# A diffusion layer on one core: third feature block's weight sums written two token steps later, second spilled chunk read back into a weight buffer

## The chip, the cores and the metric

The kernel runs on one core of one Trainium2 chip. The metric is the time of one execution on the device in microseconds (us), as the median of several runs; lower is better.

## The reference, cut to what matters

The reference is one layer of a diffusion backbone in float32: 512 latent tokens and 256 context tokens of width 1024. Each passes a gated feed-forward block, then attention and a short convolution, then a second feed-forward block. The change lies in the first feed-forward block (FFN 1, 2816 hidden features = 22 blocks of 128):

```python
def swiglu(x, w_gate, w_up, w_down):
    return (jax.nn.silu(x @ w_gate) * (x @ w_up)) @ w_down

def ffn_sublayer(h, mods, pre_g, post_g, w_gate, w_up, w_down):
    shift, scale, gate = mods
    y = swiglu(modulate(rms_norm(h, pre_g), shift, scale), w_gate, w_up, w_down)
    return h + 0.5 * gate * rms_norm(y, post_g)
```

`shift`, `scale` and `gate` come from a matrix product of the conditioning vector with `w_mod`, so the tokens can only be modulated when that product is there.

## The kernel before, in words

**Number format.** Each float32 operand of a matmul is split in two: a rounded part (`hi`, a cast on ACT, line 64) and the rest (`lo`, a subtraction, on DVE unless said otherwise, line 69). A product is then three matmuls: hi·hi, hi·lo, lo·hi.

**Start.** The 768 tokens lie transposed, as eight blocks of 128 features (k = 0 to 7). The modulation is made in four pieces of two k-blocks each: `mod_mm(i)` multiplies on PE, `mod_col(i)` turns the row into columns (eight small matmuls `pd<-pick,row` at line 351, then DVE additions into `mst` at line 356 and `s1` at line 360). `mod_x(d)` then scales block d: DVE multiplies the latent tokens (line 370), ACT adds the shift (372), POOL multiplies the context tokens (374), ACT finishes those (375), then hi and lo. `mod_t(p)` forms sums and differences of two token blocks, four products (lines 399 to 402), on POOL for p below 3, on DVE for p = 3; `mod_tp(p)` splits them into hi and lo.

The 22 hidden blocks are called f = 0 to 21. For f = 0 and 1, `open_steps` runs plain products: one `next(first)` is all matmuls (36) of one k-block. From f = 2 on, a product with seven instead of eight sub-products per 2x2 block is used. It needs sums of the weights as well: `w_load(f)` issues the two raw loads (512 KB each), `w_pool(f)` makes two sums on POOL (lines 464, 465), `w_dve(f)` two on DVE (lines 470, 471; the first needs line 464's result, and both read the raw gate weights), `w_hi(f, i)` and `w_lo(f, i)` split operand i (0 and 1 raw, 2 and 3 sums). The sum buffers `s12` and `s4` exist once each. `begin(f)` opens a block on PE, `product` is a sub-product (line 668), `plain_tail` applies Silu (line 650, with a load of ACT's table before the first) and product for f = 0 and 1 and spills the chunk.

**Order.** PE, DVE, ACT and POOL keep the order of the program text inside `with self.in_order()`. DMAs are all issued from SP; the order there is set by the framework's scheduler, as buffers come free. Inside the loop over i = 0 to 3 (lines 525 to 544), an iteration writes: k-block 2i; then for i below 3 `mod_col(i + 1)`, `mod_x` of two blocks, `mod_tp(i)`, `mod_t(i + 1)`; then k-block 2i + 1; for i below 2 `mod_mm(i + 2)`; and in i = 1 everything of f = 2's weight work that doesn't need more buffers.

**Spill and down.** Every finished hidden block f, 128 x 768 tokens as hi and lo, is written to HBM: the latent part to `hl_dram[f]` (512 KB), the context part to `hc_dram[f]`. Down (`down`, lines 764 to 789) then reads them back block by block (`fetch`, two ahead) together with a weight block `f1d[f]`, and adds into eight banks: 24 matmuls per chunk f (line 787). The chunks' read buffers are two "h" in the pool `hp`, which lives on from gate/up, and two "h2" in `fp`, which takes the memory that the gate/up pools leave at `sa.close()`. Chunk 0 is read before that (lines 740, 741) into "h", chunk 1 by `fetch(1)` into "h2". Weight blocks come through four raw buffers "wraw" of 128 x 1024, the same size as a chunk, and are split into four hi/lo pairs. Beside down's latent half DVE accumulates further modulation rows (`mod_acc`, lines 564 to 582, four steps per chunk from chunk 1 on; loads `mraw`). After it comes the context half over `hc_dram`, with the normalisation of the latent rows beside it (`sandwich`, lines 1286 to 1330).

Of the kernel before, what the change touches and what calls it, by code (L numbers as in the profile page):

```python
# [9 lines left out]
F32R = mybir.dt.float32r  # L10
# [6 lines left out]
P = 128  # L17
DM = 1024
ND = 8
NT = 512  # L20
# [19 lines left out]
class Builder:  # L40
# [153 lines left out]
    def build(self):  # L194
# [56 lines left out]
        hl_dram = self.t(dp, [NF, P, 2, NT], "hl_dram", F32R)  # L251
# [47 lines left out]
        def load_gu(f):  # L299
            out = []  # L300
            for i in range(2):
                raw = self.t(self.wp, [P, DM], "wraw", bufs=self.n_raw)
                nc.sync.dma_start(out=raw, in_=io["f1gu"][f, i])
                out.append(raw)
            return out
# [3 lines left out]
        def ring():  # L309

            i = nring[0] % 6
            nring[0] += 1
            if i < 4:
                return [self.t(self.wp, [P, DM], tag, F32R, bufs=self.n_hl) for tag in ("whi", "wlo")]
            return [self.t(fa, [P, DM], tag, F32R, bufs=2) for tag in ("whx", "wlx")]
# [89 lines left out]
        def mod_tp(p):  # L405
            u, v = tsum.pop(p)
            t12[p] = [slot(2 * p + hl, [P, 2, HK], F32R) for hl in range(2)]
            t34[p] = [self.t(fa, [P, 2, HK], "wm", F32R, bufs=8) for hl in range(2)]
            for (h, l), w in ((t12[p], u), (t34[p], v)):
                self.hi(h, w)  # L410
                self.lo(l, w, h)
# [42 lines left out]
        def w_load(f):  # L454
            rg, ru = load_gu(f)
            s12 = self.t(fa, [P, 2, 512], "s12")
            s4 = self.t(fa, [P, 512], "s4")
            wop[f] = [rg, ru, s12, s4]
            wsrc[f] = rg, ru, s12, s4

        def w_pool(f):
            rg, ru, s12, s4 = wsrc[f]
            tt = nc.gpsimd.tensor_tensor
            tt(out=s12[:, 0], in0=ru[:, :512], in1=ru[:, 512:], op=ALU.add)
            tt(out=ru[:, :512], in0=rg[:, :512], in1=ru[:, :512], op=ALU.subtract)

        def w_dve(f):
            rg, ru, s12, s4 = wsrc[f]
            tt = nc.vector.tensor_tensor
            tt(out=s12[:, 1], in0=s12[:, 0], in1=rg[:, :512], op=ALU.subtract)  # L470
            tt(out=s4, in0=rg[:, 512:], in1=s12[:, 1], op=ALU.subtract)

        def w_hi(f, i):
            raw = wop[f][i]
            raw = raw.rearrange("p s n -> p (s n)") if i == 2 else raw
            n = 512 if i == 3 else DM
            hi, lo = ring()
            self.hi(hi[:, :n], raw[:, :n])
            wop[f][i] = hi, lo, raw, n
# [34 lines left out]
        with self.in_order():  # L514
            rows = {0: mod_mm(0)}
            mod_col(0, rows.pop(0))
            gu0 = [self.split(raw, DM, ring()) for raw in raws[:2]]
            rows[1] = mod_mm(1)
            mod_x(0)
            mod_x(1)  # L520
            gu1 = [self.split(raw, DM, ring()) for raw in raws[2:]]
            mod_t(0)
            first = open_steps([gu0, gu1])
            next(first)
            for i in range(4):
                next(first)
                if i < 3:
                    mod_col(i + 1, rows.pop(i + 1))
                    mod_x(2 * i + 2)
                    mod_x(2 * i + 3)  # L530
                mod_tp(i)
                if i < 3:
                    mod_t(i + 1)
                next(first)
                if i < 2:
                    rows[i + 2] = mod_mm(i + 2)
                if i == 1:
                    w_load(2)
                    w_pool(2)
                    w_hi(2, 0)  # L540
                    w_lo(2, 0)
                    w_dve(2)
                    w_hi(2, 2)
                    w_lo(2, 2)
        ps0 = result(first)
# [132 lines left out]
        with self.in_order():  # L678
            plain_tail(0, ps0[0])
            w_hi(2, 1)  # L680
            w_lo(2, 1)
            plain_tail(1, ps0[1])
            cur = begin(2)
            w_hi(2, 3)
            w_lo(2, 3)
            tail = None
            for f in range(2, NF):
                A, K, G, (n1, n7, n6) = cur
                more = f + 1 < NF
                nc.scalar.copy(out=n1, in_=A)  # L690
                if tail:
                    product(*tail[0])
                if more:
                    w_load(f + 1)
                    w_pool(f + 1)
                    w_hi(f + 1, 0)
                    w_lo(f + 1, 0)
                if tail:
                    tail[1]()
                product(K, f, 1, 0, "t3", True)  # L700
                if more:
                    w_dve(f + 1)
                if tail:
                    tail[2]()
                nc.scalar.copy(out=n7, in_=K)
                product(A, f, 2, 1, "t2", False)
                take(mods, 3)
                if more:
                    w_hi(f + 1, 2)
                    w_lo(f + 1, 2)  # L710
                nc.scalar.copy(out=n6, in_=A)
                product(G, f, 0, 1, "b21", True)
                g = self.t(fb, [P, 2, HK], "g")
                u = self.t(fb, [P, 2, HK], "u")
                nc.vector.tensor_tensor(out=g[:, 0], in0=n1, in1=G, op=ALU.add)
                if more:
                    w_hi(f + 1, 1)
                nc.scalar.activation(g[:, 0], g[:, 0], AF.Silu)
                product(A, f, 2, 0, "t1", False)
                if more:  # L720
                    w_lo(f + 1, 1)
                nc.vector.tensor_tensor(out=u[:, 1], in0=n7, in1=A, op=ALU.add)
                product(K, f, 1, 1, "t4", False)
                if more:
                    w_hi(f + 1, 3)
                    w_lo(f + 1, 3)
                    cur = begin(f + 1)
                nc.vector.tensor_tensor(out=u[:, 0], in0=n6, in1=K, op=ALU.add)
                nc.gpsimd.tensor_tensor(out=u[:, 0], in0=u[:, 0], in1=g[:, 0], op=ALU.mult)
                take(mods, 3)  # L730

                def silu_b(g=g, u=u, A=A):
                    nc.scalar.activation(g[:, 1], A, AF.Silu)
                    nc.gpsimd.tensor_tensor(out=u[:, 1], in0=u[:, 1], in1=g[:, 1], op=ALU.mult)

                tail = ((A, f, 3, 0, "b22", False), silu_b,
                        lambda f=f, u=u: spill(f, u.rearrange("p s n -> p (s n)")))
            product(*tail[0])
            tail[1]()
            h0 = self.t(hp, [P, 2, NT], "h", F32R, bufs=2)  # L740
            self.move(h0, hl_dram[0])
            tail[2]()
            drain(mods)
            for g in ends:
                next(g, None)
# [18 lines left out]
        def down(src, n, pre, share):  # L764

            w, h = {}, dict(pre)

            def fetch(f):
                if f not in h:
                    pool, tag, bufs = (hp, "h", 2) if f % 4 in (0, 3) else (fp, "h2", 2)  # L770
                    h[f] = self.t(pool, [P, 2, n], tag, F32R, bufs=bufs)
                    self.move(h[f], src[f])
                self.pool_share = share
                w[f] = self.unit(io["f1d"][f])

            fetch(0)
            fetch(1)
            outs = yield
            for f in range(NF):
                if f + 2 < NF:  # L780
                    fetch(f + 2)
                (wh, wl), x = w.pop(f), h.pop(f)
                for d in range(ND):
                    c = slice(d * P, d * P + P)
                    o, start = outs[d]
                    for j, (wt, hl) in enumerate(((wh, 0), (wh, 1), (wl, 0))):
                        nc.tensor.matmul(o, lhsT=wt[:, c], rhs=x[:, hl], start=start and f + j == 0,  # L787
                                         stop=f == NF - 1 and j == 2, skip_group_check=True)
                yield
# [2 lines left out]
        mods = mod_late(fp, ((4, (0, 1), 4), (5, (0,), None), (8, (0,), None)))  # L792
        inorder = ExitStack()
        inorder.enter_context(self.in_order())
        part = down(hl_dram, NT, {0: h0}, 0)
        next(part)
        part.send([(p, True) for p in pl])
        for _ in part:
# [2 lines left out]
        part = down(hc_dram, NCX, {}, 3)  # L801
# [300 lines left out]
        part = {}  # L1102
# [230 lines left out]
def take(g, n):  # L1333
    for _ in range(n):
        next(g, None)
# [10 lines left out]
def drain(g):  # L1346
    for _ in g:
        pass
# [92 lines left out]
```

## Time and profile before

| what | value |
|---|---|
| median of 3 runs | 1662.25 us (1660.54 to 1670.71) |
| the profiled execution's own time | 1664.4 us |
| its span in the profile | 1662.3 us |
| PE busy | 1590.7 us (96%) |
| PE weight loads busy | 1418.7 us (85%) |
| DVE, ACT, POOL busy | 1061.0, 728.4, 274.6 us |
| mean granted PE clock | 0.982 |
| DMA | 282.20 MB, mean 170 GB/s |

The profile is of one execution. A timeline row gives start and length in us, the engine (SPq is the DMA queue of SP, and its row the issue of a transfer, not its landing), the line of the kernel, the operation with output and input, how many were merged, and in brackets how long the engine had been idle before and what ended that. In a row by windows stand, after the stretch and its length, the busy us of PE, PE's weight loads, DVE, ACT and POOL with the number of instructions, then the granted PE clock (1.00 is full), the busy share of the DMA engines and GB/s. Lines of helpers (64 for hi, 69 for lo, 74 for a move, 79 for a weight load) serve many callers; the tile's name tells which.

### The profile page before, as it was taken

The numbers are of one execution on the slowest core, as the hardware profiler recorded it, in microseconds if no ns is written. First come the engines' busy times: TensorE is split into PE (matmuls) and PEld (weight loads), VectorE is DVE, ScalarE is ACT, GpSimd is POOL, SyncE is SP. The second block draws the span as 40 slices with busy tenths as digits, with TensorE's granted clock in tenths as the row PEclk, the third lists the DMA queues.
The fourth block names the chain that finished last, engine by engine and source line by source line (L and its number), as shares of the span: only waits on it lengthen the run. The fifth ranks groups of instructions, "written<-read, shape, count | busy, mean of one in ns | idle before, by whom it ended". The sixth has DMA issues, their size and how long they took to land. (4 is left out here: it accounts for less than half of the span.)

```text
span 1662.3 us, 23526 instructions
## 1 busy us (share of the span) xinstructions
PE 1590.7 (96%) x8962; PEld 1418.7 (85%) x8962; DVE 1061.0 (64%) x1467; ACT 728.4 (44%) x1139; POOL 274.6 (17%) x204
## 2 busy tenths in 40 slices
PE   5899999998999899999999999989999999999996
PEld 4799999998888899978888888768889998888886
DVE  4598988964754785468777775575447843343335
ACT  4454445442214463436655655532247632223234
POOL 2423443431002341110000000000012100000003
PEclk9899999999999999999999999999999999999999
DMA  9054355436986764886545444745346743232321
GB/s 373 21 171 151 132 176 171 135 128 222 323 318 216 237 227 158 277 250 173 166 134 175 128 121 162 246 149 183 119 152 191 254 127 114 82 115 85 98 77 51
DMA packets 135704, 282.20 MB, mean 170 GB/s; under 512 B 22932, under 2 KB 61972, under 8 KB 135592
## 3 DMA queue, kind: packets, MB, share of 16 engines
q1 hardware_dynamic: 135592, 280.71, 52.4%
q8 instruction: 70, 1.15, 0.3%
q14 instruction: 42, 0.34, 0.1%
HBM read 229.76 MB, written 38.31 MB: 161 GB/s over the span
## 5 line engine op out<-in xcount | busy, mean ns | idle before, releaser
L64 ACT CAST whi<-wraw 128x1024 fp32r<-128x1024 f32 (+1 forms) x264 | 271.7, 1031 | 481.6 <-PE pa L109 96.9
L69 DVE TENSOR_TENSOR wlo<-wraw,whi 128x1024 fp32r<-128x1024 f32 (+1 forms) x249 | 327.5, 1317 | 181.8 <-ACT whi L64 175.4
L109 PE MATMUL f<-xs,whi 128*128 128x512 f32 x640 | 201.6, 394 | 0.2 <-DVE rq L911 0.2
L109 PE MATMUL pa<-xs,whi 128*128 128x512 f32 (+1 forms) x704 | 195.3, 361 | 0.5 <-ACT ob L1028 0.5
L787 PE MATMUL b<-h,whi 128*128 128x512 f32 (+1 forms) x704 | 178.7, 345 | 9.0 <-ACT whi L64 4.6
L787 PEld LDWEIGHTS b<-h,whi 128*128 128x128 f32 x704 | 126.5, 198 | 24.5 <-ACT whi L64 4.8
L109 PEld LDWEIGHTS pa<-xs,whi 128*128 128x128 f32 x704 | 126.0, 189 | 20.7 <-ACT ob L1028 0.7
L109 PEld LDWEIGHTS f<-xs,whi 128*128 128x128 f32 x640 | 118.2, 188 | 23.6 <-issue 0.6
L109 PE MATMUL pa<-xs,wlo 128*128 128x512 f32 (+1 forms) x352 | 126.9, 361 | 1.5 <-DVE wlo L69 1.5
L109 PE MATMUL f<-xs,wlo 128*128 128x512 f32 x320 | 125.0, 391 | 0.0
L787 PE MATMUL b<-h,wlo 128*128 128x512 f32 (+1 forms) x352 | 121.6, 345 | 0.7 <-DVE wlo L69 0.7
L109 PE MATMUL pb<-xs,whi 128*128 128x512 f32 (+1 forms) x448 | 114.4, 344 | 0.0
L580 DVE SCALAR_TENSOR_TENSOR macc<-mraw,sc,macc 128x512 f32<-128x512 f32 x112 | 93.7, 875 | 13.5 <-DMA mraw<-wmodr 13.1
L109 PEld LDWEIGHTS pb<-xs,whi 128*128 128x128 f32 x448 | 78.0, 189 | 9.9
L173 POOL TENSOR_TENSOR sqacc<-sqacc,sqt 128x256 f32<-128x256 f32 (+1 forms) x20 | 19.6, 982 | 380.1 <-ACT sqt L171 380.1
L109 PE MATMUL pb<-xs,wlo 128*128 128x512 f32 (+1 forms) x224 | 77.1, 344 | 0.0
L109 PEld LDWEIGHTS pa<-xs,wlo 128*128 128x128 f32 x352 | 66.5, 189 | 11.7 <-DVE wlo L69 1.7
L787 PEld LDWEIGHTS b<-h,wlo 128*128 128x128 f32 x352 | 69.4, 197 | 8.2 <-DVE wlo L69 1.0
L996 ACT ACTIVATE e<-s,mx 128x768 f32<-128x768 f32 x64 | 57.1, 899 | 33.7 <-DVE mx L992 33.5
L109 PEld LDWEIGHTS f<-xs,wlo 128*128 128x128 f32 x320 | 60.1, 188 | 12.7
L69 POOL TENSOR_TENSOR wlo<-wraw,whi 128x1024 fp32r<-128x1024 f32 x15 | 37.2, 2481 | 188.5 <-ACT whi L64 188.5
L909 POOL TENSOR_TENSOR rot<-rot,cossin 128x512 f32<-128x512 f32 x16 | 22.3, 1392 | 252.4 <-DVE rot L908 231.0
(363 smaller groups left out, 3604.5 us busy)
## 6 DMA issues: line engine op xcount, KB each, us to landing
mraw<-wmodr SPq DMA_DIRECT2D x56, 512.0 KB
wraw<-f2gu SPq DMA_DIRECT2D x56, 512.0 KB
wraw<-f1gu SPq DMA_DIRECT2D x44, 512.0 KB
wraw<-f1d SPq DMA_DIRECT2D x44, 512.0 KB
hl_dram<-h SPq DMA_DIRECT2D x22, 512.0 KB
h<-hl_dram SPq DMA_DIRECT2D x22, 512.0 KB
wraw<-f2d SPq DMA_DIRECT2D x24, 384.0 KB
wm<-wmod SPq DMA_DIRECT2D x16, 512.0 KB
```

The lines of the kernel that those rows point to most:

```text
L64: self.nc.scalar.copy(out=out, in_=src)
L69: (eng or self.nc.vector).tensor_tensor(out=out, in0=src, in1=hi.bitcast(F32), op=ALU.subtract)
L109: self.nc.tensor.matmul(out, lhsT=lhsT, rhs=rhs, start=start, stop=stop)
L173: eng.tensor_tensor(out=a, in0=a, in1=s, op=ALU.add)
L580: nc.vector.scalar_tensor_tensor(out=acc, in0=raw[:, k], scalar=s, in1=acc, op0=ALU.mult, op1=ALU.add)
L787: nc.tensor.matmul(o, lhsT=wt[:, c], rhs=x[:, hl], start=start and f + j == 0, stop=f == NF - 1 and j == 2, skip_group_check=True)
L909: nc.gpsimd.tensor_tensor(out=rt, in0=rt, in1=cs[:, 1, :], op=ALU.mult)
L996: nc.scalar.activation(e[m], ps[:, m * NKEY:(m + 1) * NKEY], AF.Exp, scale=SCALE, bias=mx[:, 2 + m:3 + m], accum_out=mx[:, 4 + m:5 + m])
```

## The change

In the opening loop f = 2's weight work is spread: the loads stay in iteration 1; the sums, the first split and DVE's sums go to iteration 2, behind the last modulated token blocks (k = 6 and 7) and `mod_t(3)`; the split of the first sum goes to iteration 3, behind `mod_tp(3)`. At the end of gate/up, chunk 1 is read into a raw weight buffer right behind chunk 0, and down takes it from there.

```diff
@@ -536,10 +536,12 @@
                     rows[i + 2] = mod_mm(i + 2)
                 if i == 1:
                     w_load(2)
+                if i == 2:
                     w_pool(2)
                     w_hi(2, 0)
                     w_lo(2, 0)
                     w_dve(2)
+                if i == 3:
                     w_hi(2, 2)
                     w_lo(2, 2)
         ps0 = result(first)
@@ -739,6 +741,8 @@
             tail[1]()
             h0 = self.t(hp, [P, 2, NT], "h", F32R, bufs=2)
             self.move(h0, hl_dram[0])
+            h1 = self.t(self.wp, [P, 2, NT], "wraw", F32R, bufs=self.n_raw)
+            self.move(h1, hl_dram[1])
             tail[2]()
             drain(mods)
             for g in ends:
@@ -792,7 +796,7 @@
         mods = mod_late(fp, ((4, (0, 1), 4), (5, (0,), None), (8, (0,), None)))
         inorder = ExitStack()
         inorder.enter_context(self.in_order())
-        part = down(hl_dram, NT, {0: h0}, 0)
+        part = down(hl_dram, NT, {0: h0, 1: h1}, 0)
         next(part)
         part.send([(p, True) for p in pl])
         for _ in part:
```

## The prediction

> **What bounds the kernel now.** I read busy time by stage first (windows over the whole span, here the stage of down that the argument needs and the sum: us of each engine, instructions in brackets), then the waits of PE over the span (engine, tile and line that waited, who released it; total us, times, longest us):
>
> ```profile
> 420.00:520.00 100.00, 100.00 (x445) 82.88 (x444) 56.59 (x71) 21.33 (x23) 2.39 (x1) 1.00 0.88 310
> ...
> sum 1662.30, PE 1590.69 PEld 1418.68 DVE 1061.00 ACT 728.36 POOL 274.59; mean PE 122.36 PEld 109.13 DVE 81.62 ACT 56.03 POOL 21.12
> ```
>
> ```profile
> PE pa L157 <- ACT xe L64: 10.5, 2, 7.0
> ...
> PE b L787 <- DMA h<-hl_dram: 4.3, 1, 4.3
> ```
>
> PE bounds: it is busy for 1590.7 of 1662.3 us, so 71.6 us of idle time are all there is to win, and what a halved clock costs. The change touches both of these waits. **First place, 71 to 97 us** (timeline of PE, then DVE, POOL, ACT; columns: start, us, engine, line, operation, idle time before it):
>
> ```profile
> 52.79 0.95 PE L157 MATMUL pd<-pick,row 128*128 128x2 f32 x8
> ...
> 65.49 0.95 PE L157 MATMUL pd<-pick,row 128*128 128x2 f32 x8
> ...
> 71.10 0.33 PE L157 MATMUL pc<-xo,wlo 128*128 128x256 f32 x1
> 78.46 0.69 PE L157 MATMUL pa<-xe,whi 128*128 128x384 f32 x1 [7.03 <-ACT xe L64]
> ...
> 97.21 0.61 PE L668 MATMUL pa<-xs,whx 128*128 128x384 f32 x2 [0.68 <-ACT n L690]
> ```
>
> ```profile
> 53.77 0.36 DVE L356 TENSOR_TENSOR mst<-pd,vec 128x2 f32<-128x2 f32 x4 [3.09 <-PE pd L157]
> ...
> 58.58 0.75 DVE L370 SCALAR_TENSOR_TENSOR xs<-xs,s,pbs 128x512 f32<-128x512 f32 x1
> ...
> 63.21 0.95 DVE L69 TENSOR_TENSOR wm<-sqt,wm 128x768 fp32r<-128x768 f32 x1
> 64.37 1.75 DVE L69 TENSOR_TENSOR wlx<-wraw,whx 128x1024 fp32r<-128x1024 f32 x1 [0.21 <-ACT whx L64]
> 70.23 0.69 DVE L470 TENSOR_TENSOR s<-s,wraw 128x512 f32<-128x512 f32 x1 [4.10 <-POOL s L464]
> 70.95 1.65 DVE L471 TENSOR_TENSOR s<-wraw,s 128x512 f32<-128x512 f32 x1
> ...
> 74.19 0.35 DVE L356 TENSOR_TENSOR mst<-pd,vec 128x2 f32<-128x2 f32 x4
> ```
>
> ```profile
> 65.12 1.87 POOL L400 TENSOR_TENSOR sqt<-xs,sqt 128x384 f32<-128x384 f32 x1
> ...
> 67.93 1.01 POOL L402 TENSOR_TENSOR sqt<-xs,sqt 128x384 f32<-128x384 f32 x1
> 68.90 1.29 POOL L464 TENSOR_TENSOR s<-wraw 128x512 f32<-128x512 f32 x1
> 70.27 1.79 POOL L465 TENSOR_TENSOR wraw<-wraw,wraw 128x512 f32<-128x512 f32 x1
> ```
>
> PE finishes k-block 5 at 71.43 (4.99 us behind the eight small matmuls of 65.49) and starts block 6 at 78.46. Its tokens (mod_x(6)) hang on the modulation columns that PE delivers from 65.49. DVE picks them up (L356) only at 74.19; for the earlier pair it took 0.98 us (52.79 to 53.77). In between stands feature 2's weight work in program order: the wlx at 64.37, then L470, which waits for POOL's sum L464 behind mod_t's four products, L471 and a second wlx. So the columns lie 74.19 − 66.47 = 7.7 us on DVE's queue.
>
> **Second place, the change from gate/up to down** (PE, then the DMA queue SP):
>
> ```profile
> 397.92 0.39 PE L787 MATMUL b<-h,wlo 128*128 128x512 f32 x1
> 402.64 1.22 PE L787 MATMUL b<-h,whi 128*128 128x512 f32 x2 [4.33 <-DMA h<-hl_dram]
> ...
> 410.80 0.61 PE L787 MATMUL b<-h,whi 128*128 128x512 f32 x2
> ...
> 416.24 0.61 PE L787 MATMUL b<-h,whi 128*128 128x512 f32 x2
> ```
>
> ```profile
> 354.77 0.33 SPq L79 DMA_DIRECT2D wraw<-f1d  x1
> ...
> 379.57 0.33 SPq L74 DMA_DIRECT2D h<-hl_dram  x1
> ...
> 398.55 1.53 SPq L74 DMA_DIRECT2D h<-hl_dram  x3
> ```
>
> Chunk 0 (issued 379.57) is there in time. Chunk 1 is one of three reads issued from 398.55, when chunk 0's matmuls are already done, and arrives 402.64 − 398.55 = 4.1 us later. Two 1 us windows show what the idle time does to PE's clock (the third number from the end):
>
> ```profile
> 401.00:402.00 1.00, 0.00 (x0) 0.00 (x0) 0.00 (x0) 0.00 (x0) 0.00 (x0) 0.69 1.02 381
> ...
> 408.00:409.00 1.00, 1.00 (x6) 0.83 (x5) 1.00 (x2) 0.00 (x0) 0.00 (x0) 0.90 0.18 70
> ```
>
> It halves 3.1 us after PE stopped (0.69 = full until 401.38) and is full again at 408.2, 5.6 us after the restart.
>
> **The change, second part first: h1 early.** It adds and removes no work: one 512 KB read moves up, from fp's "h2" buffer to a raw weight buffer. In the new program it stands right behind chunk 0's read and ahead of the last spill. A raw buffer comes free at 354.77 (there goes the first f1d load), so nothing behind h1 on SP waits for it, and it lands before 398. Chunk 1's matmuls then start where chunk 0's end, one pitch behind the last: 398.16. The loads of their weights begin at 354.77 too. Chunk 2 now starts at 398.16 + 5.44 = 403.6 (5.44 = 416.24 − 410.80, a full-clock chunk) instead of 410.80: **7.2 us**, of which 4.5 are the wait and 2.7 the halved clock (410.80 − 402.64 = 8.16 against 5.44). What is late next: chunk 2's read goes with the group at 398.55 and, at chunk 1's 4.1 us, lands at 402.6, 1.0 before its need.
>
> The price: a raw buffer is held until 403.6. If the ring goes strictly round, the load of chunk 3's weights needs just this buffer: issue at 403.7, 4.1 us like the read above, 1.05 for ACT's cast, and it is ready at 408.9 to 410.2 (with DVE's 1.23) against a need of 409.05: 0 to 1.2 us late. DVE's accumulations stand behind that cast, and further on the casts' lead is small:
>
> ```profile
> 406.45 0.88 DVE L577 TENSOR_SCALAR macc<-mraw,sc 128x512 f32<-128x512 f32 x2 [9.43 <-DMA mraw<-wmodr]
> ...
> 497.52 3.49 DVE L69 TENSOR_TENSOR wlo<-wraw,whi 128x1024 fp32r<-128x1024 f32 x3
> ```
>
> At 497.52 the casts of three chunks come; the first serves chunk 19, due at 416.24 + 16 × 5.44 = 503.28, a lead of 4.6 us after its 1.2. If the accumulations did not move up with PE, 7.2 − 4.6 = 2.6 would be lost there. I expect them to move up: a chunk has four accumulations (0.88 for two at 406.45) and a low part of 1.2 on DVE, about 3 us in 5.44. If the ring takes whichever buffer is free, all this is nothing. I take 0.3 off: **6.9**, bounds 3.4 (both lost) and 7.2, or 0 if the read doesn't move.
>
> **First part: the weight sums behind the last tokens.** Nothing is added; POOL's two products, three casts and subtractions change places. I walk the queues from 65.49. L356 at 66.47, the first L370 at 67.3. POOL's L402 ends at 68.05 (68.94 less the 0.87 by which the wlx held L400, 1.87 against about 1.0). POOL and DVE hold each other up when both read two SBUF operands: L471, 0.69 by L470, took 1.65 beside L465. So L370 runs 68.05 to 68.8, POOL's two small products (0.57 each: 1.89 less DVE's 0.75, next row) to 69.95, L464 to 71.2. The low parts of block 6 on DVE, ready at 70.6, wait for it (71.2 to 71.8), the other half for L465 (1.3, to 73.1), and L370 of block 7 starts at 73.6.
>
> ```profile
> 54.52 1.89 POOL L374 TENSOR_TENSOR xs<-xs,pbs 128x256 f32<-128x256 f32 x2
> ```
>
> ```profile
> 86.42 0.55 DVE L402 TENSOR_TENSOR pbs<-xs,sqacc 128x384 f32<-128x384 f32 x1
> 87.40 0.96 DVE L69 TENSOR_TENSOR xs<-sqacc,xs 128x768 fp32r<-128x768 f32 x1 [0.43 <-ACT xs L64]
> ...
> 93.24 1.23 DVE L69 TENSOR_TENSOR wlo<-wraw,whi 128x1024 fp32r<-128x1024 f32 x1
> ```
>
> ```profile
> 88.44 1.28 ACT L650 ACT_TABLE_LOAD   x1 [0.33 <-DVE xs L69]
> 89.73 0.60 ACT L650 ACTIVATE g<-pa 128x512 f32<-128x512 f32 x1
> ```
>
> From L370 to the end of that group the earlier pair took 64.16 − 58.58 = 5.6: 79.2. mod_t(3), four products like L402, starts 0.5 apart: 81.2. Here the moved work now lies: wlx 1.2, L470 and L471 1.3, then mod_tp(3)'s 0.9: 84.6. ACT's table load waits for exactly this instruction (88.36 to 88.44), and the first Silu follows 1.29 later: **86.0 instead of 89.73**. PE doesn't bound here: block 6 loses some 2 us to the late low parts and block 7 ends at 83.1, then PE idles 3.5 us. From the first Silu the chain over ACT and DVE takes 97.21 − 89.73 = 7.48 us to where PE runs on without a stall. A new wait lies in it: feature 3's L464 and L465 on POOL wait for the sum buffer s12 (one buffer), released by the moved wlx(2) at 86.6; they run to 89.6 and hold DVE's low parts back by about 1.0. So that matmul comes at 86.0 + 7.5 + 1.0 = 94.5 instead of 97.21: **2.7 us**. Bounds: with no hold anywhere the Silu comes at 83.8 and the gain is 5.9; with L464 and L465 (1.29 + 1.79) both in the way, 3.7 − 3.1 = 0.6. The raw load that waits for L471 goes some 11 us later, but serves feature 4; f2's own load stays.
>
> The half clock after the 3.5 us idle lasts, by the 5.6 above, until 92.1. The product that needs wlo(2,1) starts at about 91.7, so it loses 0.2, hidden.
>
> [...]
>
> **Sum:** 2.7 + 6.9 = 9.6 us. The profiled execution took 1664.4 around its span of 1662.3, which would become 1654.8. The runs' median, 1662.25, lies 2.2 lower, so **1652.6 us**, 0.6% less. Behind 416 us I expect all to shift as it is: from 420 to 520 PE never idles.
>
> **The rivals.** (a) The ring goes strictly round and both prices fall due: 3.4 + 2.7 = 6.1, 1656.1. For it: four raw buffers, one held. Against: a buffer that comes free earlier may be handed out first. (b) The change doesn't do what it says for h1: SP's order isn't the program's (the f1d load of 354.77 stands later in the program than the read of 379.57), and the read could again land behind the last spill. Only 2.7 is left: 1659.5. Against: its buffer and its data are ready early. (c) A stall further on goes away too:
>
> ```profile
> 555.51 2.73 SPq L1315 DMA_DIRECT2D h_dram<-yl  x2
> ...
> 559.76 0.42 SPq L79 DMA_DIRECT2D wraw<-f1d  x1
> ```
>
> ```profile
> 564.92 0.57 PE L787 MATMUL b<-h,whi 128*128 128x256 f32 x2 [4.63 <-ACT whi L64]
> ```
>
> A weight load stands on SP behind two stores that wait for DVE. If SP's order there is drawn anew and the load goes first, 4.6 and about 2.7 of clock go: 1645.3. (d) The same the other way, **slower**: in the context half of down (520 to 570) two more weight loads come to stand behind waiting stores, each 7.3: 1652.6 + 14.6 = 1667.2. It decides from the second such load on; one leaves 1659.9. Against: engines are pinned to program order there.
>
> **How the numbers follow.** Forecast 0.5, (a) 0.2, (b) 0.12, (c) 0.1, (d) 0.08. The likeliest's own range is 1649 (5.9 + 7.2) to 1658 (0.6 + 3.4). The range for 8 in 10 takes in (a), (b) and almost (c): 1646 to 1661. A measurement of this kernel tells about 1% (16.6 us) from no change; only (c) with a good first part passes it: 0.07. Slower by over 1% needs (d) twice over: 0.03. Within 1%: 0.90.
>
> **What would show it.** Right: PE starts block 6 near 71.5 with a short wait for DVE, the first Silu comes near 86, PE idles before begin(2); no wait for h at chunk 1, and from the matmul now at 97.21 to chunk 2's start at 410.80 it is 306.4 to 306.7 us instead of 313.6. Wrong: that distance unchanged (h1 late), the Silu after 89, a new PE wait for whi or wlo between 403 and 510 us, or a changed wait in 520 to 570.

## The result, and the profile after

The changed kernel takes a median of 1652.68 us against 1663.67 of the kernel before beside it, nine runs of each; two of the changed kernel's nine (1766.73 and 4030.30) were disturbed and are left out of the ratio, and the median of its other seven is 1651.96. The **ratio is 0.993, 95% interval 0.9914 to 0.9945**, so 9 to 14 us less. Two repetitions on other chips gave 0.9929 (0.991 to 0.9947) and 0.9915 (0.9898 to 0.9933). The forecast was 1652.6. The profiled execution took 1653.65 around a span of 1650.9. Line numbers are two higher behind the first edit and four behind the second: before's L668, L650, L690 and L787 are now L670, L652, L692 and L791.

The waits of PE over the span (total us, times, longest):

```profile
PE b L791 <- ACT whi L64: 4.8, 1, 4.8
...
PE pa L157 <- ACT xe L64: 3.5, 1, 3.5
PE pa L670 <- ACT g L652: 3.4, 1, 3.4
...
PE pa L157 <- DVE h L69: 1.1, 1, 1.1
```

The wait of 7.0 for block 6's tokens is gone (of the two waits for `xe` the other, 3.5, remains), and so is the 4.3 for `h`. New are a wait of 3.4 before `begin(2)` and one of 1.1 inside block 6. The wait for a weight cast behind the stores stays (4.8; 4.6 before).

**First place.** PE, then DVE, POOL and ACT:

```profile
66.46 0.95 PE L157 MATMUL pd<-pick,row 128*128 128x2 f32 x8
...
74.10 0.33 PE L157 MATMUL pa<-h,whi 128*128 128x128 f32 x1 [1.10 <-DVE h L69]
...
86.91 0.62 PE L670 MATMUL pa<-xe,whx 128*128 128x384 f32 x2 [3.37 <-ACT g L652]
...
95.00 0.57 PE L670 MATMUL pa<-xs,whx 128*128 128x384 f32 x2
```

```profile
67.44 0.36 DVE L356 TENSOR_TENSOR mst<-pd,vec 128x2 f32<-128x2 f32 x4 [2.32 <-PE pd L157]
...
68.09 1.46 DVE L370 SCALAR_TENSOR_TENSOR xs<-xs,s,pbs 128x512 f32<-128x512 f32 x1
...
72.42 1.63 DVE L69 TENSOR_TENSOR h<-xs,h 128x384 fp32r<-128x384 f32 x1
73.97 0.74 DVE L370 SCALAR_TENSOR_TENSOR xs<-xs,s,pbs 128x512 f32<-128x512 f32 x1
...
83.94 0.95 DVE L69 TENSOR_TENSOR xs<-sqacc,xs 128x768 fp32r<-128x768 f32 x1
...
88.81 1.63 DVE L69 TENSOR_TENSOR h<-g,h 128x768 fp32r<-128x768 f32 x1 [0.90 <-ACT h L64]
```

```profile
70.81 1.27 POOL L464 TENSOR_TENSOR s<-wraw 128x512 f32<-128x512 f32 x1
72.16 1.47 POOL L465 TENSOR_TENSOR wraw<-wraw,wraw 128x512 f32<-128x512 f32 x1
86.97 1.29 POOL L464 TENSOR_TENSOR s<-wraw 128x512 f32<-128x512 f32 x1 [13.35 <-DVE wlx L69]
88.34 1.29 POOL L465 TENSOR_TENSOR wraw<-wraw,wraw 128x512 f32<-128x512 f32 x1
```

```profile
86.26 0.60 ACT L652 ACTIVATE g<-pa 128x512 f32<-128x512 f32 x1
```

This execution reached the eight small matmuls 0.97 later than the one before (66.46 against 65.49), so times are read from there. DVE takes the columns up after 0.98 us instead of 8.7. The first Silu comes 19.80 after the small matmuls (before 24.24), and the first free-running matmul 28.54 after them (before 31.72): **3.2 us** won. The low part of block 6 lies beside POOL's L465 (1.63 for what took 0.55 in a quiet place), and feature 3's L465 (88.34 to 89.63) holds the low part at 88.81 (1.63, where the same one took 0.96 at 92.29 before).

**Second place.** PE and the queue of SP:

```profile
390.44 0.63 PE L791 MATMUL b<-h,whi 128*128 128x512 f32 x2
...
395.92 0.62 PE L791 MATMUL b<-wraw,whi 128*128 128x512 f32 x2
...
401.36 0.62 PE L791 MATMUL b<-h,whi 128*128 128x512 f32 x2
```

```profile
352.55 0.33 SPq L74 DMA_DIRECT2D wraw<-hl_dram  x1
...
377.34 0.33 SPq L74 DMA_DIRECT2D h<-hl_dram  x1
...
394.11 0.53 SPq L74 DMA_DIRECT2D hl_dram<-h  x1
```

Chunk 1 is read at 352.55, ahead even of chunk 0 (377.34), and chunk 2 starts 10.92 after chunk 0 where it took 410.80 − 392.67 = 18.13 (392.67: chunk 0's first matmul before): **7.2 us**. By windows, before and then after (columns as in the prediction):

```profile
40.00:100.00 60.00, 51.50 (x382) 48.11 (x382) 35.89 (x59) 29.28 (x45) 21.35 (x18) 0.91 0.21 70
390.00:420.00 30.00, 25.67 (x106) 21.15 (x105) 13.95 (x24) 4.48 (x5) 2.02 (x2) 0.89 0.67 245
```

```profile
40.00:100.00 60.00, 54.22 (x397) 50.78 (x397) 38.94 (x65) 31.50 (x48) 19.87 (x18) 0.94 0.25 84
390.00:420.00 30.00, 30.00 (x135) 24.89 (x134) 17.28 (x30) 6.59 (x7) 1.31 (x2) 1.00 0.78 278
420.00:510.00 90.00, 90.00 (x399) 74.53 (x398) 51.38 (x64) 18.75 (x20) 2.40 (x1) 1.00 0.91 327
```

In the second row PE is without a gap and at full clock. Up to 510 us no wait follows.

**The whole pair.** The spans differ by 1662.3 − 1650.9 = 11.4 us: −0.97 (the later start) + 3.18 + 7.23 = 9.44, and 2.0 that the edits don't touch (7.23 is taken from the free-running matmul to chunk 2: 313.59 less 306.36). Further on both kernels wait for the same row (1.77 us until 1265.20 before, 1.76 until 1255.99 after). From chunk 2's start to this row it is 854.40 us before and 854.63 after, so the 2.0 lies behind it. There the clock halved before (1264.94 to 1271.78) and didn't after. Five us behind the row, before and after:

```profile
1266.00:1271.00 5.00, 5.00 (x24) 5.00 (x25) 2.93 (x8) 2.21 (x5) 0.10 (x1) 0.50 0.94 300
```

```profile
1256.00:1261.00 5.00, 5.00 (x42) 5.00 (x43) 4.75 (x10) 3.11 (x8) 0.74 (x1) 1.00 0.99 337
```

### The profile page after: what moved, and what is told of

Read it like the earlier page. It is cut to its first block, busy times and chain, and to the rows that moved or that the text cites. A ratio compares the mean times of both kernels' runs of the same rounds, so it can differ in the third digit from the quotient of the medians.

```text
span 1650.9 us, 23528 instructions
## 1 busy us (share of the span) xinstructions
PE 1585.6 (96%) x8962; PEld 1414.2 (86%) x8962; DVE 1061.0 (64%) x1467; ACT 727.8 (44%) x1139; POOL 272.0 (16%) x204
## 5 line engine op out<-in xcount | busy, mean ns | idle before, releaser
L791 PE MATMUL b<-h,whi 128*128 128x256 f32 (+1 forms) x688 | 172.0, 341 | 4.8 <-ACT whi L64 4.8
L791 PEld LDWEIGHTS b<-h,whi 128*128 128x128 f32 x688 | 122.3, 196 | 18.9 <-ACT whi L64 5.0
L791 PE MATMUL b<-h,wlo 128*128 128x256 f32 (+1 forms) x344 | 117.4, 341 | 0.7 <-DVE wlo L69 0.7
L582 DVE SCALAR_TENSOR_TENSOR macc<-mraw,sc,macc 128x512 f32<-128x512 f32 x112 | 93.8, 876 | 10.4 <-DMA mraw<-wmodr 10.1
L109 PEld LDWEIGHTS pa<-xs,wlo 128*128 128x128 f32 x352 | 66.5, 189 | 11.6 <-DVE wlo L69 1.7
L791 PEld LDWEIGHTS b<-h,wlo 128*128 128x128 f32 x344 | 67.5, 196 | 7.6 <-DVE wlo L69 1.0
```

The source lines that it names most:

```text
L109: self.nc.tensor.matmul(out, lhsT=lhsT, rhs=rhs, start=start, stop=stop)
L582: nc.vector.scalar_tensor_tensor(out=acc, in0=raw[:, k], scalar=s, in1=acc, op0=ALU.mult, op1=ALU.add)
```

## The experiments

Two lengths serve as rulers in all runs: S, from the eight small matmuls (66.46 in the changed kernel) to the first free-running matmul (95.00), and D, from chunk 0's first matmul of down to the first of the context half. Before: S 31.72, D 126.93. Changed: S 28.54, D 119.72. "Silu" is its distance from the small matmuls.

| kernel | median us (runs) | ratio to before, 95% | Silu | S | D |
|---|---|---|---|---|---|
| first edit alone | 1660.99 (12) | 0.9976 (0.9963 to 0.9989) | 19.88 | 28.35 | 127.05 |
| second edit alone | 1656.24 (6) | 0.9954 (0.9939 to 0.9969) | 24.26 | 31.74 | 119.72 |
| POOL's sums earlier | 1655.14 (5) | 0.9935 (0.9922 to 0.9949) | 19.27 | 28.01 | 119.72 |
| shorter queue as well | 1654.47 (5) | 0.9935 (0.9922 to 0.9948) | 18.15 | 26.98 | 119.72 |
| changed kernel again | 1653.44 (6) | 0.9929 (0.991 to 0.9947) | 19.82 | 27.88 | 119.72 |
| read written in down | 1652.15 (4) | 0.9923 (0.9903 to 0.9942) | 19.82 | 27.88 | 119.72 |
| two chunks held | 1654.96 (4) | 0.9929 (0.9907 to 0.9951) | 19.83 | 27.89 | 119.72 |
| stores on POOL | 1653.68 (6) | 0.9929 (0.9912 to 0.9946) | 19.85 | 28.59 | 119.72 |
| late stores on ACT | 1648.72 (6) | 0.9897 (0.9879 to 0.9915) | 19.80 | 27.86 | 119.72 |
| late stores on SP | 1649.62 (6) | 0.9897 (0.9879 to 0.9914) | 19.80 | 27.85 | 119.72 |
| changed kernel, third | 1652.06 (6) | 0.9915 (0.9898 to 0.9933) | 19.80 | 27.86 | 119.73 |

Rows 1 to 4 shared a chip (before 1664.88), then rows 5 to 8 (1664.18) and 9 to 11 (1666.24).

### Each edit alone

The first kernel has the first part of the change's diff alone, the second the two others:

```diff
                 if i == 1:
                     w_load(2)
+                if i == 2:
                     w_pool(2)
...
+                if i == 3:
                     w_hi(2, 2)
```

```diff
+            h1 = self.t(self.wp, [P, 2, NT], "wraw", F32R, bufs=self.n_raw)
+            self.move(h1, hl_dram[1])
...
-        part = down(hl_dram, NT, {0: h0}, 0)
+        part = down(hl_dram, NT, {0: h0, 1: h1}, 0)
```

> The kernel before with the first edit alone (weight sums written behind the last tokens), chunk 1 read as before. My theory (two separate stalls, each worth its own part): counted from the start C of the last eight small column matmuls on PE, the first Silu comes at C + 19.8 us as in the changed kernel (24.2 before) and the first matmul that runs on without a stall (sum operand 2 on the token differences) at C + 28.5 (31.7 before); the wait of about 4.3 us for chunk 1 and the half clock behind it stay, so chunk 2 starts 18.1 us behind chunk 0. Time 3 us below the kernel before: about 1660.5, ratio 0.998. Rival (the first edit does nothing for the end, the work is only moved in front of the Silu): ratio 1.000 and C + 31.7.

> The kernel before with the second edit alone (chunk 1 read early into a raw weight buffer). My theory: the stall of 7 us at k-block 6 stays (Silu at C + 24.2), chunk 2 starts 10.9 us behind chunk 0 instead of 18.1, nothing is lost later: 7.2 us below the kernel before, about 1656.5, ratio 0.9957. Rival (the held raw buffer costs part of it): chunk 3 or a later one waits for its weight block, and the ratio is 0.998 or more.

The rulers move one by one: with the first edit alone S falls and D stays, with the second alone the other way round. The remaining wait with the first edit alone, PE:

```profile
400.64 1.22 PE L789 MATMUL b<-h,whi 128*128 128x512 f32 x2 [4.38 <-DMA h<-hl_dram]
```

By the ratios the first edit brings 0.24% (4.0 us, interval 1.8 to 6.2) and the second 0.46% (7.7 us, 5.2 to 10.2). Together that is 0.70%, what the changed kernel gives. As far as these intervals and the two rulers tell, the edits are independent.

### What holds the first edit back: POOL's sums earlier, then a shorter queue on DVE

The first of these two puts the load one iteration earlier and POOL's sums ahead of `mod_t(2)`; the second puts, on top of that, DVE's sums behind `mod_t(2)`, the two casts behind the modulation in iteration 2, and the low parts later:

```diff
                 if i < 3:
                     mod_col(i + 1, rows.pop(i + 1))
...
+                if i == 1:
+                    w_pool(2)
...
-                if i == 1:
+                if i == 0:
                     w_load(2)
                 if i == 2:
-                    w_pool(2)
```

```diff
+                if i == 1:
+                    w_dve(2)
+                if i == 3:
+                    w_lo(2, 0)
...
-                    w_lo(2, 0)
-                    w_dve(2)
-                if i == 3:
...
-                    w_lo(2, 2)
...
+            if f == 0:
+                w_lo(2, 2)
```

> The changed kernel, with feature 2's raw load written one iteration earlier and POOL's two sums ahead of mod_t(2) in iteration 1, in a stretch where POOL idles. My theory (POOL's sums hold up DVE's low parts of k-block 6, 1.11 and 1.63 us instead of 0.55 each): both low parts take 0.55 again, PE's wait of 1.1 us at k-block 6 goes, the Silu comes 1.6 us earlier, at C + 18.2, and the time is 1 to 2 us lower than the changed kernel's. Rival (DVE's own queue alone sets the Silu and the holds are hidden): Silu at C + 19.8 as before, time the same.

> As the run before this, and DVE's sums of feature 2 in iteration 1 too (DVE idles there while it waits for the columns), ACT's two casts of feature 2 in iteration 2, and DVE's subtractions behind the last token sums and behind the first products of the Silu. So nothing of feature 2 stands on DVE in front of the instruction that the Silu's table load waits for. My theory (that queue sets the Silu): Silu at C + 16.2, the first matmul that runs on at C + 24.6 to 25, PE idles under 2 us before block 2 and keeps its full clock; about 3.5 to 4 us below the changed kernel, 1649, ratio to the kernel before 0.991. Rival (the chain behind the Silu and the clock set the end, not the Silu): Silu at C + 16.2 too, but the matmul not before C + 27, and the time within 1.5 us of the changed kernel's.

Both miss. With POOL's sums earlier, DVE and POOL:

```profile
67.65 1.47 DVE L370 SCALAR_TENSOR_TENSOR xs<-xs,s,pbs 128x512 f32<-128x512 f32 x1
71.89 0.56 DVE L69 TENSOR_TENSOR xe<-xs,xe 128x384 fp32r<-128x384 f32 x1 [2.77 <-ACT xe L64]
72.37 0.55 DVE L69 TENSOR_TENSOR h<-xs,h 128x384 fp32r<-128x384 f32 x1
```

```profile
68.52 1.47 POOL L402 TENSOR_TENSOR sqt<-xs,sqt 128x384 f32<-128x384 f32 x1
69.95 1.42 POOL L374 TENSOR_TENSOR xs<-xs,pbs 128x256 f32<-128x256 f32 x2
```

The low parts are quiet again (0.56, 0.55), as the theory had it. But POOL's `mod_t(2)` now ends 4.12 us after the small matmuls instead of 2.55. Its last product is held too (L402, 1.47 for 1.0), beside the DVE instruction that starts block 6 (L370, 1.47 for 0.75, as the 1.46 in the changed kernel). So POOL's L374 comes later, and ACT, which the forecast of this run left out, waits for it. Only 0.5 us of the expected 1.6 is left. The shorter queue brings DVE's sums between POOL's products. DVE:

```profile
64.98 1.49 DVE L470 TENSOR_TENSOR s<-s,wraw 128x512 f32<-128x512 f32 x1
66.51 1.39 DVE L471 TENSOR_TENSOR s<-wraw,s 128x512 f32<-128x512 f32 x1
67.82 0.35 DVE L356 TENSOR_TENSOR mst<-pd,vec 128x2 f32<-128x2 f32 x4
...
86.98 2.30 DVE L69 TENSOR_TENSOR wlo<-wraw,whi 128x1024 fp32r<-128x1024 f32 x1
```

L470 and L471 take 2.88 instead of 1.37, so L356 comes 2.55 after the small matmuls instead of 0.98, and later `wlo` is held by feature 3's sums. S falls to 26.98, 1.6 less than in the changed kernel's own profile (0.9 less than in its repetitions), and the times of both kernels don't differ from it measurably. In both orders tried, two-operand work of DVE still lay beside POOL's somewhere: moving the work moved the hold.

### Does the place in the program or the buffer bring chunk 1 early? Does a held buffer cost anything?

The first kernel reads chunk 1 from down's own loop over the chunks, but into a raw weight buffer; the second holds chunk 2 in one as well:

```diff
-            h1 = self.t(self.wp, [P, 2, NT], "wraw", F32R, bufs=self.n_raw)
-            self.move(h1, hl_dram[1])
...
+                    if f == 1 and n == NT:
+                        pool, tag, bufs = self.wp, "wraw", self.n_raw
...
-        part = down(hl_dram, NT, {0: h0, 1: h1}, 0)
+        part = down(hl_dram, NT, {0: h0}, 0)
```

```diff
+            h2 = self.t(self.wp, [P, 2, NT], "wraw", F32R, bufs=self.n_raw)
+            self.move(h2, hl_dram[2])
...
-        part = down(hl_dram, NT, {0: h0, 1: h1}, 0)
+        part = down(hl_dram, NT, {0: h0, 1: h1, 2: h2}, 0)
```

> The changed kernel itself once more, beside the kernel before and the runs below on one chip. Both theories: ratio 0.993, some 11 us below the kernel before; from block 0's first down matmul to the context half 119.7 us, from there to the last matmul 1131 to 1135 us, depending on where the halved clock falls.

> The changed kernel, with chunk 1's read written at its old place in the program (the second fetch of down, behind the last spill), into a raw weight buffer. My theory (it is the buffer, free long before, that lets the read go early, not the place in the program): the read is issued before 380 us, chunk 2 starts 10.9 us behind chunk 0, time as the changed kernel. Rival (the place in the program decides): the read goes behind the last spill again, near 396 us, chunk 1 waits some 4 us and 7 us are lost.

> The changed kernel, with chunk 2 too read early into a second raw weight buffer: two of four raw buffers held. It doubles the suspected cost; chunk 2 came in time anyway, so there is nothing to win. My theory (the weight loads run so far ahead that a held buffer costs nothing): no wait of PE for weights between chunk 0 and the context half, 119.7 us from one to the other, time as the changed kernel. Rival (held buffers cost weights): PE waits at chunk 3 or 4 for a cast, 1 us or more, or at chunks 17 to 19.

With the read written in down, where it stood before, but into a raw weight buffer, SP still issues it some 37 us ahead of the last spill:

```profile
355.69 0.33 SPq L74 DMA_DIRECT2D wraw<-hl_dram  x1
...
392.34 0.53 SPq L74 DMA_DIRECT2D hl_dram<-h  x1
```

D is 119.72 again. So the **buffer** decides, not the line in the program: in the kernel before, "h2" didn't exist until gate/up's memory was given back. With two of four raw buffers held, PE has no gap either:

```profile
390.00:420.00 30.00, 30.00 (x134) 24.83 (x133) 20.18 (x33) 6.10 (x6) 0.77 (x1) 1.00 0.85 302
420.00:508.00 88.00, 88.00 (x390) 72.87 (x389) 48.19 (x61) 18.77 (x20) 2.39 (x1) 1.00 0.90 322
```

The price that the prediction put on the held buffer isn't there. (This kernel's median is 1.5 above the repetition's, with D the same to 0.01 and both ratios 0.9929. The difference lies further on, and four runs against six don't tell it from scatter.)

### The stall behind the stores (the prediction's rival c)

First the stores of the latent rows go to POOL (in the latent rows' call alone):

```diff
-                    nc.sync.dma_start(out=h_out[d], in_=y[d])
+                    (nc.gpsimd if late_st else nc.sync).dma_start(out=h_out[d], in_=y[d])
```

> The changed kernel, with the stores of the normalised latent rows (eight of 256 KB beside the context half of down) issued by POOL instead of SP. My theory (the stall of 4.8 us that stands in both kernels at the context half comes from a weight load that stands on SP behind two waiting stores): the wait of PE for the cast goes from 4.8 to under 1 us, no half clock behind it, some 5 to 7 us below the changed kernel, about 1646. Rival (the load waits for its raw buffer or for the memory, not for SP's order): the wait stays at 4 us or more, or moves to another load, and the time stays within 2 us.

The wait for the cast went and another came, PE, DVE and POOL:

```profile
558.24 0.73 PE L109 MATMUL b<-mraw,ones_r 128*128 128x512 f32 x2 [4.62 <-ACT macc L598]
```

```profile
552.58 4.48 DVE L173 TENSOR_TENSOR sqacc<-sqacc,sqt 128x512 f32<-128x512 f32 x1
```

```profile
552.92 1.29 POOL L173 TENSOR_TENSOR sqacc<-sqacc,sqt 128x512 f32<-128x512 f32 x1
554.15 2.35 POOL L69 TENSOR_TENSOR wlo<-wraw,whi 128x1024 fp32r<-128x1024 f32 x1
```

A DVE addition of 0.68 lasts 4.48: it spans POOL's addition and the low part behind it, up to 556.50. ACT's next square waits for it (557.09), and the row copy that PE waits for stands behind that square (557.63). Two such additions before it last 4.50 and 3.40; the longest in this stretch of the changed kernel lasts 2.25. That is the same hold as above, read from the rows and not tested by itself. What the experiment shows is that POOL, which has its own work between the stores, was the wrong place for them here. That left another cure: don't store a row the moment it is made. Two kernels store it two steps later, on ACT, or with `nc.sync` in the same place on SP:

```diff
-                if h_out is not None:
-                    nc.sync.dma_start(out=h_out[d], in_=y[d])
             if d >= lag:
+                if h_out is not None:
+                    nc.scalar.dma_start(out=h_out[d - lag], in_=y[d - lag])
                 self.sqadd(pool, sq2, y[d - lag], d - lag, T)
```

> The changed kernel, with the eight stores of the latent rows in the context half issued by ACT, each two steps later (just ahead of the squares of the same row, which ACT waits for anyway). Theory: no queue then waits for DVE with a weight load behind it, and no more work stands beside POOL than in the changed kernel. The wait of PE for a weight cast (4.8 us in the changed kernel) goes, and no wait of over 2 us takes its place between 520 and 570 us; from the first 128x256 matmul of the context half the kernel is 4 to 7 us shorter: 1646 to 1649. Rival: the stall only moves again, as with the stores on POOL (a DVE or ACT wait of 4 to 5 us in 540 to 570 us): 1652 to 1655.

> The same two steps of delay, with the stores still issued by SP. Theory: SP then waits for rows that are nearly always done, so the weight loads behind it go in time and the result is that of the stores on ACT: no PE wait for a weight cast, 1646 to 1649. Rival: the order on SP, not how late the row is, keeps the load back (the loads stand behind stores whose rows still wait for DVE): the wait of 4 to 5 us stays and the time with it, 1652 to 1655.

> The changed kernel itself beside the two others on one chip: 1651 to 1655, with the wait of PE for a weight cast of 4 to 5 us between 520 and 570 us.

Windows of the changed kernel (third), of the stores on ACT and of those on SP:

```profile
520.00:570.00 50.00, 45.41 (x350) 43.77 (x349) 36.60 (x46) 24.62 (x36) 22.72 (x10) 0.97 0.79 258
```

```profile
520.00:570.00 50.00, 49.85 (x395) 48.95 (x395) 43.75 (x53) 29.09 (x42) 24.09 (x12) 0.97 0.90 296
```

```profile
520.00:570.00 50.00, 48.38 (x387) 46.97 (x386) 41.12 (x50) 27.70 (x41) 23.78 (x11) 1.00 0.83 275
```

The third profile of the changed kernel misses what was expected of it: its wait for the cast is 0.89, not 4 to 5.

```profile
550.54 0.50 PE L791 MATMUL b<-h,whi 128*128 128x256 f32 x2 [0.89 <-ACT whi L64]
```

In the changed kernel's three profiles this wait is 4.80, 2.59 and 0.89 us; the last two have a wait of 1.61 and 1.83 for a chunk besides, whose read goes out on SP right behind a store (538.21, the store at 537.49). So the stall is made up of several waits, and their sizes change from one execution to the next. PE's idle time in the stretch falls from 4.6, the four waits of the third profile together, to 0.2 and 1.6, and no wait over 1 us takes their place. From the start of the context half to PE's last matmul it is 1126.8 and 1125.8 us, against 1130.0 in the changed kernel beside them (1130.3 and 1131.0 in its other two profiles). The medians are 3.3 and 2.4 us lower. The gain is shown by the traces; the intervals of the ratios still overlap with the changed kernel's own. Of the expected 4 to 7 us they reach the low end at most; in the profile beside them the stall had cost little clock (0.97 over the stretch, where the changed kernel's first profile has 0.88). So the late stores beat the kernel before by 1.0% and the changed kernel by some 3 us, the latter by traces and medians alone. It is the lateness that matters here, not the queue: on SP, where the stores were before, the gain differs from ACT's by less than the medians can tell.

## Why the prediction was right

**Second edit: right, and a term too many.** Forecast 7.2 less 0.3 for a held buffer, measured 7.2. The read went out as soon as a raw buffer was free (352.55), even ahead of reads written before it, and no weight cast came late. The free buffer is handed out and the ring isn't strictly round: seven weight loads went out from 357.45 on and before chunk 0 began (390.44), while chunk 1 held its buffer until it was used (395.92 to 401.36). A strict ring of four would have stopped after three. Two held buffers cost nothing either. Rival (a) falls with that. Rival (b), the read behind the last spill, falls by 352.55 against 394.11. From the free-running matmul to chunk 2 it is 401.36 − 95.00 = 306.4 us, as the prediction wanted to see.

**First edit: mechanism right, three sizes off that partly cancel.** Forecast 2.7, measured 3.2 in the profiled pair and 3.8 in the repetition (31.72 − 27.88).
- *The Silu*, forecast at 86.0 − 65.49 = 20.5 after the small matmuls, came at 19.8. L464 came where it was put (4.35 after them, forecast 4.46). The held low part was over by 74.05, 0.4 after POOL's L465, and block 7's L370 began at 7.51 instead of 8.1. That 0.6 carries through.
- *The hold by feature 3's sums*, forecast "about 1.0", was 0.67: one low part, 1.63 at 88.81 where the quiet row has 0.96. The next one, `wlo`, behind L465's end, was not held (1.21 at 90.37).
- *The half clock* was forecast to lie from the restart to 92.1 and to cost a hidden 0.2. It lay elsewhere, and its place decides 0.7 us. The changed kernel's profile, then its repetition's:

```profile
88.00:89.00 1.00, 1.00 (x6) 1.00 (x5) 0.19 (x1) 1.00 (x2) 0.92 (x2) 0.64 0.82 299
...
94.00:95.00 1.00, 1.00 (x5) 1.00 (x4) 0.97 (x2) 1.00 (x2) 0.00 (x0) 0.50 1.05 171
95.00:96.00 1.00, 1.00 (x7) 1.00 (x7) 0.75 (x1) 0.70 (x2) 0.00 (x0) 0.94 0.94 375
```

```profile
85.00:86.00 1.00, 0.55 (x2) 0.55 (x3) 1.00 (x2) 0.67 (x2) 0.49 (x1) 0.79 0.87 209
...
88.00:89.00 1.00, 1.00 (x4) 1.00 (x4) 1.00 (x2) 1.00 (x3) 0.16 (x1) 0.50 0.80 324
89.00:90.00 1.00, 0.71 (x4) 0.39 (x3) 1.00 (x1) 0.03 (x1) 0.00 (x0) 1.00 0.06 25
```

In the one, PE restarts at 86.91, the clock halves at 88.28 and is full at 95.12 (6.84 us), and the product behind it loses 0.7 (S 28.54 against 27.88). In the other it is half from 85.58 to 89.00 (3.42), under the product at the restart, behind which PE waits for DVE anyway, and nothing is lost. The same program and the same 3.4 us of idle time gave both. Eight profiles have this opening: the changed kernel's three and the five with edits further on. In two of them the half clock lasts to 94.7 or 95.1, and S is 28.54 and 28.59; in six it is over by 90.5, and S is 27.85 to 27.89. So the 5.6 of the prediction was no fixed time from a restart: from the restart to full clock it was 8.2 us in the one (86.91 to 95.12) and 3.6 in the other (85.45 to 89.00). What these stretches have in common is in the last section.

**The rest.** 3.2 to 3.8 and 7.2 make 10.4 to 11.0, against 0.7% of 1663.67 = 11.6, inside its interval. The forecast of 9.6 was low by the 0.3 and by 0.5 to 1.1 in the first part. That the median lies within 0.1 us of the forecast is luck: the kernel before came out 1.4 higher over nine runs than over the three that the forecast started from, and the gain came out 1.4 higher than the sum. Rivals (c) and (d) both needed a new order of SP's loads beside the stores: the stall there was 4.6 before and 4.8 after, and the loads stood behind the two stores as before, so neither came. (In the changed kernel's third profile the order is the same and the wait for the cast 0.89, so a changed wait there would not have shown either rival by itself.) The later runs show that (c) named a real stall, with some 3 us to win, though not by this change.

## What to carry to other kernels

A prefetch can be late for want of its buffer and not for its place in the program: look for a buffer of another pool, of the same size, that comes free earlier, and ask whether the pool hands out the free one. Work put behind the critical instruction in an engine's order gains the wait, less what that work now holds up elsewhere; with DVE and POOL both on two-operand work, look at the rows beside each place it could go, for here the hold moved along with it (a low part of 0.96 took 1.63 beside POOL's sum, DVE's two sums 2.88 instead of 1.37). Stores that waited for their rows kept the loads behind them on SP waiting: try writing such a store a step or two late.

## What the runs showed of the hardware

- **Each half-clock stretch named here lasted one, two or three times about 3.41 us.** It lasted 6.82 us (29.32 to 36.14 and 401.38 to 408.20 before), 10.24 (73.70 to 83.94 before), 6.84 (88.28 to 95.12 after) and 3.42 (85.58 to 89.00, the repetition). Read from windows of 1 us, all 14 changes of the clock before, from 29.32 to 1271.78 us, stand within 0.02 us of whole multiples of 3.4133 us behind the first (1242.46 us are 364 of them). The changed kernel's eleven, from 30.26 to 1641.35 us, do the same from a start of their own (1611.09 us are 472 of them). In the profile after, the clock halved when PE had already restarted: 4.7 us after PE stopped and 1.4 after it ran again (83.54, 86.91, 88.28).
- **The same wait cost clock in one profile and none in the other.** With the 1.8 us wait (until 1265.20 before, 1255.99 after) the clock was half for 6.84 us before (1264.94 to 1271.78, about 2 us lost) and stayed full after. That it depends on where the wait falls among these multiples is the author's estimate from these figures; no run sets it on purpose. A single pair of profiles of this kernel isn't good to better than about 2 us.
